# Layer 0's mixer takes x feature-major from the host, and squares the later token rows behind the value copies

## The chip, the cores and the metric

One core of one Trainium2 chip. The metric is the device time of one execution in microseconds (us). The engines are TensorE (PE, with its weight loads as PEld), VectorE (DVE), ScalarE (ACT), GpSimd (POOL) and SyncE (SP), which here issues nearly all DMAs.

## What is computed

A decoder trunk of two layers over 1024 tokens of width 1024, float32. Each layer is a token mixer and a gated feed-forward part with a causal convolution, each behind an RMS norm and with a residual. The change touches the beginning of layer 0's mixer: the norm of x, and the projections to q, k and v of the attention.

```python
def rms_norm(x, g):
    xf = x.astype(jnp.float32)
    return xf * lax.rsqrt(jnp.mean(xf * xf, -1, keepdims=True) + EPS) * g.astype(jnp.float32)
...
    z = h @ w_in
    u, v, q, k, vb = jnp.split(
        z, [A_WIDTH, 2 * A_WIDTH, 2 * A_WIDTH + B_WIDTH, 2 * A_WIDTH + 2 * B_WIDTH], axis=-1)
...
    qh = rms_norm(heads(q), q_g)
    kh = rms_norm(heads(k), k_g)
    vh = heads(vb).astype(jnp.float32)
```

## The kernel before

A float32 product is made of three products of shorter numbers. `split` (L95) writes a high part (a cast, on ACT unless `hi` names another engine, L100) and a low part (the difference, on DVE, L101); `mm_tok` (L182, matmuls at L190) multiplies high by high, high by low and low by high. The norm's weight is folded into the projection's weights (`scaled`, L103, rows L105 on ACT and L106 on DVE), and the norm's factor of each token (`r0`, one column for each of the 8 tiles of 128 tokens) is applied to the projection's result.

`even` (L510) begins with a loop over the 8 token tiles. For each it loads 128 rows of x (L523), turns them with 8 transposes on PE into two PSUM banks (`pt`, L530), splits each bank into `hq` (L531, 4 x 128 columns for each of two groups `g`), and sums the squares of the rows on ACT (L536); POOL makes the factor from the sum (`inv_rms`, L140 and L141). In the tile 1 round the weights of head pair 0 are loaded and split (`load_qkv`).

`attention` (L643) loads the q and k norm weights into `gqk` (four DMAs, L647 and L648, two copies of each side by side), scales the q part (L649), and calls `project(0, wq0)`. `project` (L696) goes over the 8 token tiles: 24 matmuls make `pj` of 128 x 384 (q, k, v of two heads); ACT squares q and k (L712), DVE sums them by head (L714), POOL makes the factor `rq`, DVE applies it (L716), POOL multiplies by `gqk` (L718), ACT copies the values to `vN` (L720), which a DMA writes out (L721). POOL and DVE split q and k into `qs` and `ks`, PE turns them (`tq` L730, `tk` L738; one PSUM bank for both), ACT or DVE copy them out (`qT` L733, `kT` L739), and `unit` makes scores `sc` (L661), the softmax (L666 on DVE, L667 on ACT), its transposes `pP` (L681), their copy `pT` and the products with the values `po` (L689). In `pj`, tile n of head pair p is written `pj{p}{n}`; buffer numbers are left out in the profile.

Each engine works off its own instructions in the order in which a scheduler put them when the program was built; that order is in the program, and an instruction that waits holds up all behind it on its engine. SP issues DMAs in order too.

Of the kernel before, what the change touches and what calls it, by code (L numbers as in the profile page):

```python
# [9 lines left out]
F32 = mybir.dt.float32  # L10
# [3 lines left out]
AF = mybir.ActivationFunctionType  # L14
# [5 lines left out]
P = 128  # L20
# [30 lines left out]
def rows(t, n):  # L51
    return t[n * P : (n + 1) * P, :]
# [3 lines left out]
def trunk(ctx: ExitStack, tc: tile.TileContext, a, out):  # L56
# [41 lines left out]
    def split(dst, src, hi=None, lo=None):  # L98

        (hi or A.copy)(dst[0], src)  # L100
        (lo or V.tensor_sub)(dst[1], src, f32(dst[0]))  # L101
# [65 lines left out]
    def place(t, n):  # L167
        return [t[:, i, :, (n % 4) * P : (n % 4 + 1) * P] for i in range(2)]
# [340 lines left out]
    def even(gm_open):  # L509
        with ExitStack() as st:  # L510
# [8 lines left out]
            pq0 = par0.enter_context(tc.tile_pool(name="pq0", bufs=1, side="right", reuse_waits="tile"))  # L519
            with tc.tile_pool(name="nrm", bufs=1, reuse_waits="tile") as pool:  # L520
                for n in range(NT):
                    xt = pool.tile([P, D], F32, tag="x", bufs=3, name=f"x0{n}")
                    Q.dma_start(xt, rows(a["x"], n))  # L523
                    if n == 0:
                        Q.dma_start(g0, a["norm_mix_gT"])
                    for g in range(2):
                        pt = ps.tile([P, 4, P], F32, tag="pt", name=f"pt{n}{g}")
                        for j in range(4):
                            k = 2 * j + g
                            T.transpose(pt[:, j, :], xt[:, k * P : (k + 1) * P], ident)  # L530
                        split(place(hq[g][n // 4], n), pt)  # L531
                    if n == 1:
                        wq0 = load_qkv(0, wx)
                    h = pool.tile([P, D], F32, tag="h", bufs=2, name=f"h{n}")
                    ssq = small.tile([P, 1], F32, tag="ssq", name=f"ssq{n}")
                    A.activation(h, xt, AF.Square, accum_out=ssq)  # L536
                    inv_rms(ssq, 1, D, f"rn{n}", r0[:, n : n + 1])
            with tc.tile_pool(name="at", bufs=2, reuse_waits="tile") as at, \
                    tc.tile_pool(name="av", bufs=1, reuse_waits="tile") as av:
                return attention(ps, at, av, pq, pq0, par0, wx, wq0, masks, gm_open)  # L540

# [100 lines left out]

    def attention(ps, at, av, pq, pq0, par0, wx, wq0, masks, gm_open):  # L643

        gqk = pq.tile([P, 2, 2, 64], F32, name="gqk", bufs=1)
        for s in range(2):
            Q.dma_start(gqk[:, 0, s, :], a["q_g"].partition_broadcast(P))  # L647
            Q.dma_start(gqk[:, 1, s, :], a["k_g"].partition_broadcast(P))  # L648
        V.tensor_scalar(gqk[:, 0], gqk[:, 0], -0.125, None, op0=ALU.mult)  # L649
        gqk = gqk.rearrange("p a s c -> p (a s c)")  # L650
        mband, mboth = masks
# [43 lines left out]

        def project(p, ws=None, then=None):  # L696

# [7 lines left out]
            for n in range(NT):  # L705
# [11 lines left out]
                                       op0=ALU.mult, op1=ALU.mult)  # L717
                G.tensor_tensor(qn, qn, gqk, op=ALU.mult)  # L718
                vN.append(pq.tile([P, P], F32, tag="vN", bufs=3, name=f"vN{p}{n}"))
                A.mul(vN[n], pj[:, 256:384], rn)  # L720
                Q.dma_start(rows(vd, n), vN[n])  # L721
# [78 lines left out]

        made = project(0, wq0)
        for p in range(PAIRS):
# [404 lines left out]
def layouts(i):  # L1207
# [26 lines left out]
    def tiles(w):  # L1234
# [4 lines left out]
    return {n: c(v) for n, v in {  # L1239
        "x": A["x"][0],  # L1240
        "norm_mix_g": A["norm_mix_g"][1:],
        "norm_mix_gT": A["norm_mix_g"][0].reshape(KD, P).T,
# [40 lines left out]
```

## Time and profile before

| what | value |
|---|---|
| three timed runs | 2170.96, 2171.78 (median) and 2174.12 us |
| the profiled execution | 2173.38 us, of which 2171.7 us are the profile's span |
| PE busy | 2138.3 us, 98% of the span |
| DVE, ACT, POOL busy | 71%, 48%, 23% |

The profile names a group of instructions by line, engine, operation and tiles (out<-in). In a list by time the columns are start, duration, engine, line, operation, tiles, count, and in brackets how long the engine had been idle and what ended it. In a table by stretch of time each engine has its busy time and count; then come the clock that TensorE was granted, the share of the DMA engines, and GB/s. An instruction's time is that of the hardware's record; those of one engine overlap a little, so the distance of two starts can be shorter than a duration.

### The profile page before, as it was taken

Reading aid. Unit: us, or ns where it says so; the run is one execution under the profiler, and the core shown is the slowest. Engines: PE = TensorE matmul, PEld = TensorE weight load, DVE = VectorE, ACT = ScalarE, POOL = GpSimd, SP = SyncE. Lnnn points to the kernel's source line nnn. Section 1 sums busy time; section 2 is a strip of 40 time slices with the busy share of each in tenths; the row PEclk is TensorE's granted clock in tenths of the full one; section 3 lists DMA queues with packets and bytes.
Section 4 is the critical chain, followed back from the end, with each engine's and each line's share of the span. In section 5 each row is a group of like instructions: output and inputs, shape, how many; then the busy total and the mean of one; then the engine's idle time right before and its main releaser. Section 6 shows DMA issues by size and latency. Waiting matters only on the chain.

```text
span 2171.7 us, 29864 instructions
## 1 busy us (share of the span) xinstructions
PE 2138.3 (98%) x10508; PEld 1811.4 (83%) x10508; DVE 1533.7 (71%) x2451; ACT 1033.9 (48%) x1998; POOL 488.9 (23%) x519
## 2 busy tenths in 40 slices
PE   8999999999999999999999999999999999999999
PEld 7999988887888888878889888888788888888887
DVE  6566655577887888755577776667788878885554
ACT  6555545355444444444454455534544444444443
POOL 4444411012342434100020011110233424220000
PEclk9999999999999999999999999999999999999999
DMA  4122312655444444675563233386554444457555
GB/s 163 43 83 62 82 51 84 217 207 193 159 151 160 160 165 160 199 266 195 193 215 127 73 98 97 107 295 232 197 165 160 151 152 157 165 181 276 199 196 202
DMA packets 157254, 349.59 MB, mean 161 GB/s; under 512 B 17408, under 2 KB 54272, under 8 KB 156720
## 3 DMA queue, kind: packets, MB, share of 16 engines
q1 hardware_dynamic: 157104, 347.68, 47.6%
q8 instruction: 83, 1.36, 0.3%
q14 instruction: 67, 0.55, 0.1%
HBM read 239.02 MB, written 108.59 MB: 160 GB/s over the span
## 4 chain that ended last, share of the span: by engine, by line
PE 87%; DVE 4%; DMA 4%; ACT 3%; issue 1%; POOL 0%; SPq 0%; ACTq 0%; DVEq 0%; POOLq 0%
PE puB L290 11%; PE pgB L290 11%; PE pv L190 6%; PE pgC L290 6%; PE puC L290 6%; PE pj L190 5%; PE pdB L397 5%; PE pdC L397 5%; PE po L190 4%; PE pdO L397 4%; PE puA L290 3%; PE pgA L290 3%; PE pdP L397 2%; PE pdQ L397 2%; PE pu L190 2%; PE pBq L992 2%
## 5 line engine op out<-in xcount | busy, mean ns | idle before, releaser
L101 DVE TENSOR_TENSOR da<-ar,da 128x512 fp32r<-128x512 f32 x154 | 106.2, 690 | 160.2 <-ACT da L100 160.1
L100 ACT CAST da<-ar 128x512 fp32r<-128x512 f32 x154 | 95.9, 623 | 215.0 <-PE pdQ L397 91.8
L190 PE MATMUL po<-wo,hq 128*128 128x512 f32 x768 | 184.3, 395 | 1.2 <-ACT hq L100 1.2
L190 PEld LDWEIGHTS po<-wo,hq 128*128 128x128 f32 x768 | 141.6, 188 | 30.9 <-ACT hq L100 1.6
L190 PE MATMUL pv<-wv,hq 128*128 128x512 f32 (+2 forms) x768 | 139.8, 339 | 2.0 <-DVE b L1024 1.6
L397 PE MATMUL pdB<-dw,da 128*128 128x512 f32 x528 | 136.3, 391 | 2.4 <-ACT dw L100 1.7
L397 PE MATMUL pdC<-dw,da 128*128 128x512 f32 x528 | 135.8, 390 | 0.0
L190 PEld LDWEIGHTS pv<-wv,hq 128*128 128x128 f32 x768 | 118.9, 189 | 17.4 <-DVE b L1024 2.1
L397 PEld LDWEIGHTS pdB<-dw,da 128*128 128x128 f32 x528 | 98.6, 188 | 24.0 <-ACT dw L100 2.1
L190 PE MATMUL pj<-wq,hq 128*128 128x384 f32 x576 | 117.3, 346 | 0.2 <-ACT vN L720 0.2
L256 POOL TENSOR_TENSOR S1g<-rg 128x512 f32<-128x512 f32 x20 | 30.0, 1498 | 382.9 <-DMA wsd<-D 249.7
L397 PEld LDWEIGHTS pdC<-dw,da 128*128 128x128 f32 x528 | 99.1, 188 | 20.5
L101 DVE TENSOR_TENSOR dw<-wr,dw 128x512 fp32r<-128x512 f32 x154 | 105.6, 686 | 8.2 <-ACT dw L100 7.7
L140 POOL TENSOR_SCALAR rn<-ssq 128x1 f32<-128x1 f32 x24 | 9.6, 399 | 452.2 <-ACT h L148 246.0
L397 PE MATMUL pdO<-dw,da 128*128 128x512 f32 x396 | 102.3, 389 | 0.2 <-DVE dw L101 0.2
L190 PEld LDWEIGHTS pj<-wq,hq 128*128 128x128 f32 x576 | 100.3, 191 | 0.5 <-ACT vN L720 0.4
L100 ACT CAST dw<-wr 128x512 fp32r<-128x512 f32 x154 | 95.0, 617 | 11.9 <-DMA wr<-in_w_dn 5.0
L397 PEld LDWEIGHTS pdO<-dw,da 128*128 128x128 f32 x396 | 74.3, 188 | 15.9 <-DVE dw L101 0.6
L319 DVE SCALAR_TENSOR_TENSOR t<-g,cw,t 128x1022 f32<-128x1022 f32 x44 | 76.6, 1742 | 0.1
L318 DVE SCALAR_TENSOR_TENSOR t<-g,cw,t 128x1023 f32<-128x1023 f32 x44 | 60.2, 1368 | 16.3 <-ACT t L317 16.3
L303 DVE TENSOR_TENSOR g<-g,s1g 128x512 f32<-128x512 f32 x22 | 16.2, 737 | 76.7 <-ACT s1g L302 76.7
L320 ACT ACTIVATE t<-t 128x1024 f32<-128x1024 f32 x44 | 46.7, 1061 | 32.5 <-DVE t L319 32.5
(1073 smaller groups left out, 5458.7 us busy)
## 6 DMA issues: line engine op xcount, KB each, us to landing
ar<-actd SPq DMA_DIRECT2D x70, 512.0 KB, 3.6
rd<-in_w_down SPq DMA_DIRECT2D x44, 512.0 KB, 3.7
wsd<-D SPq DMA_DIRECT2D x88, 256.0 KB, 2.5
rg<-in_w_gate SPq DMA_DIRECT2D x42, 512.0 KB, 3.6
ru<-in_w_up SPq DMA_DIRECT2D x42, 512.0 KB, 4.7
wr<-wsd SPq DMA_DIRECT2D x40, 512.0 KB, 4.3
actd<-t SPq DMA_DIRECT2D x66, 256.0 KB, 2.2
wr<-in_w_dn SPq DMA_DIRECT2D x30, 512.0 KB, 4.6
```

The source lines that it names most:

```text
L100: (hi or A.copy)(dst[0], src)
L101: (lo or V.tensor_sub)(dst[1], src, f32(dst[0]))
L140: G.tensor_scalar(r, ssq, 1.0 / n, EPS, op0=ALU.mult, op1=ALU.add)
L190: T.matmul(o, L[i], R[jj][:, sl], start=(k == 0 and (ii, jj) == PASSES[0]), stop=(k == nk - 1 and (ii, jj) == PASSES[-1]))
L256: G.tensor_tensor(sums[name], x, y, op=op)
L290: T.matmul(o, L[ii][:, j * P : j * P + P], right[p][:, jj, j, :], skip_group_check=more, start=(not more and j == 0 and (ii, jj) == PASSES ...
L303: V.tensor_add(C22, C22, s1)
L318: V.scalar_tensor_tensor(t[:, 1:], g[:, : S - 1], w(1), t[:, 1:], op0=ALU.mult, op1=ALU.add)
L319: V.scalar_tensor_tensor(t[:, 2:], g[:, : S - 2], w(0), t[:, 2:], op0=ALU.mult, op1=ALU.add)
L320: A.activation(t, t, AF.Silu)
L397: T.matmul(o, L[ii][:, t * P : t * P + P], R[jj], skip_group_check=more, start=start and not more and (ii, jj) == PASSES[0], stop=stop and ...
L992: T.matmul(o, L[ii][:, j * P : j * P + P], right[p][:, jj, j, :], skip_group_check=more, start=(not more and j == 0 and (ii, jj) == PASSES ...
```

## The change

The host hands over a second copy of x, `x_T`, in the form that `hq` needs. The first loop loads a tile of it (`xf`, L544) and splits it straight from the loaded tile; the transposes and their PSUM banks are gone. For tiles 0 to 3 the high part of the second group is a copy on POOL. The token rows of x are loaded as well (`token_rows`, L535), since the sums of squares need them: those of tiles 0 to 2 are squared in the loop, in place; those of tiles 3 to 7 wait in memory that head pair 1 uses later (`xk`, `xq`), and `rest` puts their squares behind the copy of the values of tile n - 3 in `project`. The q and k norm weights are loaded once each, into one copy (`gains`), and the multiplication on POOL (now L744) reads them for both heads through an operand that repeats.

```diff
             with tc.tile_pool(name="nrm", bufs=1, reuse_waits="tile") as pool:
+                Q.dma_start(g0, a["norm_mix_gT"])
+                xk = pq.tile([P, 4, S], F32, tag="kT", bufs=1, name="xk")
+                xq = pq.tile([P, 2, S], F32, tag="qR", bufs=1, name="xq")
+
+                def home(name, tag, bufs):
+                    return pool.tile([P, D], F32, tag=tag, bufs=bufs, name=name)
+
+                def statistics(n, xt):
+                    ssq = small.tile([P, 1], F32, tag="ssq", name=f"ssq{n}")
+                    A.activation(xt, xt, AF.Square, accum_out=ssq)
+                    inv_rms(ssq, 1, D, f"rn{n}", r0[:, n : n + 1])
+
+                def token_rows(n):
+                    xt = home(f"x0{n}", "a", 6) if n < 3 else xk[:, n - 3] if n < 7 else xq[:, 1]
+                    Q.dma_start(xt, rows(a["x"], n))
+                    later.append(xt)
+                    if n < 3:
+                        statistics(n, xt)
+
+                later = []
                 for n in range(NT):
-                    xt = pool.tile([P, D], F32, tag="x", bufs=3, name=f"x0{n}")
-                    Q.dma_start(xt, rows(a["x"], n))
+                    xt = home(f"xf{n}", "a", 6) if n < 4 else home(f"xf{n}", "b", 2) if n < 6 else xq[:, n - 6]
+                    xf = xt.rearrange("p (g j t) -> p g j t", g=2, j=4)
+                    Q.dma_start(xf, a["x_T"][n])
+                    for g in range(2):
+                        split(place(hq[g][n // 4], n), xf[:, g], hi=G.tensor_copy if g and n < 4 else None)
                     if n == 0:
-                        Q.dma_start(g0, a["norm_mix_gT"])
-                    for g in range(2):
-                        pt = ps.tile([P, 4, P], F32, tag="pt", name=f"pt{n}{g}")
-                        for j in range(4):
-                            k = 2 * j + g
-                            T.transpose(pt[:, j, :], xt[:, k * P : (k + 1) * P], ident)
-                        split(place(hq[g][n // 4], n), pt)
-                    if n == 1:
                         wq0 = load_qkv(0, wx)
-                    h = pool.tile([P, D], F32, tag="h", bufs=2, name=f"h{n}")
-                    ssq = small.tile([P, 1], F32, tag="ssq", name=f"ssq{n}")
-                    A.activation(h, xt, AF.Square, accum_out=ssq)
-                    inv_rms(ssq, 1, D, f"rn{n}", r0[:, n : n + 1])
+                        token_rows(0)
+                    elif n > 1:
+                        if n == 2:
+                            gqk = gains(pq)
+                        token_rows(n - 1)
+                token_rows(NT - 1)
+
+            def rest(n, ins):
+                if n < 5:
+                    with tc.issue_after(ins.ins):
+                        statistics(n + 3, later[n + 3])
...
+    def gains(pq):
+
+        gqk = pq.tile([P, 2, 64], F32, name="gqk", bufs=1)
+        Q.dma_start(gqk[:, 0], a["q_g"].partition_broadcast(P))
+        Q.dma_start(gqk[:, 1], a["k_g"].partition_broadcast(P))
+        V.tensor_scalar(gqk[:, 0], gqk[:, 0], -0.125, None, op0=ALU.mult)
+        return gqk
...
-        gqk = pq.tile([P, 2, 2, 64], F32, name="gqk", bufs=1)
-        for s in range(2):
-            Q.dma_start(gqk[:, 0, s, :], a["q_g"].partition_broadcast(P))
-            Q.dma_start(gqk[:, 1, s, :], a["k_g"].partition_broadcast(P))
-        V.tensor_scalar(gqk[:, 0], gqk[:, 0], -0.125, None, op0=ALU.mult)
-        gqk = gqk.rearrange("p a s c -> p (a s c)")
...
-                G.tensor_tensor(qn, qn, gqk, op=ALU.mult)
+                both = qn.rearrange("p (a s c) -> p a s c", a=2, s=2)
+                G.tensor_tensor(both, both, gqk[:, :, None, :].to_broadcast([P, 2, 2, 64]), op=ALU.mult)
                 vN.append(pq.tile([P, P], F32, tag="vN", bufs=3, name=f"vN{p}{n}"))
-                A.mul(vN[n], pj[:, 256:384], rn)
+                got = A.mul(vN[n], pj[:, 256:384], rn)
+                if early:
+                    early(n, got)
...
-        made = project(0, wq0)
+        made = project(0, wq0, early=rest)
...
         "x": A["x"][0],
+        "x_T": A["x"][0].reshape(NT, P, 4, 2, P).transpose(0, 4, 3, 2, 1),
```

The order of the instructions changes on every engine up to the first matmul of head pair 1 (`pj` of pair 1, tile 0); from there on each engine has the same instructions in the same order as before. Three places of the changed part follow; a name's number tells buffers apart.

SP's queue at the start of the program, before: x's tiles 0 and 1 stand ahead of the weights of pair 0 (`wq00r` to `wq03r`).

```order
L523 DMA x_324<-in_x 128x1024
L525 DMA g_83<-in_norm_mix_gT 128x8
L523 DMA x_346<-in_x 128x1024
L110 DMA wq00r<-in_w_qkv 128x768
L110 DMA wq01r<-in_w_qkv 128x768
L110 DMA wq02r<-in_w_qkv 128x768
L110 DMA wq03r<-in_w_qkv 128x768
L523 DMA x_399<-in_x 128x1024
L647 DMA gqk<-in_q_g 128x64
```

The same place now (`xf` is a tile of `x_T`, `x` one of token rows):

```order
L521 DMA g_83<-in_norm_mix_gT 128x8
L544 DMA xf_327<-in_x_T 128x1024
L110 DMA wq00r<-in_w_qkv 128x768
L110 DMA wq01r<-in_w_qkv 128x768
L110 DMA wq02r<-in_w_qkv 128x768
L110 DMA wq03r<-in_w_qkv 128x768
L535 DMA x_365<-in_x 128x1024
L544 DMA xf_371<-in_x_T 128x1024
L544 DMA xf_377<-in_x_T 128x1024
L568 DMA gqk<-in_q_g 128x64
L569 DMA gqk<-in_k_g 128x64
L535 DMA x_387<-in_x 128x1024
```

The weights now stand behind one tile instead of two, the second tile behind the weights and the first token rows, and x goes through the queue twice.

On PE, where the turning of q and k of tile 0 begins, before: transposes of x stand between `tq`, `tk` and the scores (`pj_773` is tile 3, `pj_852` tile 4).

```order
L190 MATMUL pj_773<-wq_0_388,hq_85 128x384 x3
L738 MATMUL tk_590<-identr,ks_579 128x128 x3
L530 MATMUL pt_471<-ident,x_462 128x128 x4
L738 MATMUL tk_590<-identr,ks_579 128x128
L190 MATMUL pj_773<-wq_1_391,hq_87 128x384 x3
L530 MATMUL pt_485<-ident,x_483 128x128 x4
L190 MATMUL pj_852<-wx_364,hq_86 128x384 x3
```

Now `tq`, `tk` and the scores of tile 0 stand side by side between tiles 2 and 3 (`pj_604` and `pj_686`):

```order
L190 MATMUL pj_604<-wq_1_362,hq_87 128x384 x3
L758 MATMUL tq_489<-identr,qs_483 128x128 x2
L766 MATMUL tk_495<-identr,ks_484 128x128 x4
L686 MATMUL sc0n_504<-kT_440,qT_492 128x128 x2
L686 MATMUL sc0n_511<-kT_440,qT_492 128x128 x2
L190 MATMUL pj_686<-wx_335,hq_85 128x384 x3
```

What stood between the steps of one tile is gone from there.

On DVE, ahead of the copy of the keys of tile 1 (`kT_440<-tk_575`), now; the `hq` row has the loaded tile `xq` as input, and weights of pair 1 (`wq_0_1276` and on) stand in the row:

```order
L101 TENSOR_TENSOR qs_645<-qn_629,qs_645 128x2x64
L101 TENSOR_TENSOR hq_88<-xq,hq_88 128x4x128
L106 SCALAR_TENSOR_TENSOR wq_0_1276<-wq10r,g_83,wq_0_1276 128x384
L101 TENSOR_TENSOR ks_646<-qn_629,ks_646 128x2x128
L711 COPY pT0n_518<-pP0n_503 128x2x128
L106 SCALAR_TENSOR_TENSOR wq_1_1279<-wq10r,g_83,wq_1_1279 128x384
L739 TENSOR_REDUCE ss_713<-qn_711 128x4
L106 SCALAR_TENSOR_TENSOR wq_0_1284<-wq11r,g_83,wq_0_1284 128x384
L106 SCALAR_TENSOR_TENSOR wq_1_1287<-wq11r,g_83,wq_1_1287 128x384
L741 SCALAR_TENSOR_TENSOR qn_711<-pj_686,r_84,rq_715 128x256
L739 TENSOR_REDUCE ss_796<-qn_794 128x4
L767 CAST kT_440<-tk_575 128x16x32
```

Before, the same copy stood behind these:

```order
L101 TENSOR_TENSOR hq_88<-pt_492,hq_88 128x4x128
L101 TENSOR_TENSOR qs_810<-qn_798,qs_810 128x2x64
L101 TENSOR_TENSOR hq_86<-pt_506,hq_86 128x4x128
L739 CAST kT_539<-tk_666 128x16x32
```

The four weights of pair 1 (`wq10r`, `wq11r`), which before stood far ahead of it, have moved to just in front of this copy.

More of the change, by code (lines that the diff above doesn't have):

```diff
@@ L538, in even @@
+                token_rows(NT - 1)
[3 more added lines that the diff above has]
+                        statistics(n + 3, later[n + 3])
             with tc.tile_pool(name="at", bufs=2, reuse_waits="tile") as at, \
                     tc.tile_pool(name="av", bufs=1, reuse_waits="tile") as av:
-                return attention(ps, at, av, pq, pq0, par0, wx, wq0, masks, gm_open)
+                return attention(ps, at, av, pq, pq0, par0, wx, wq0, gqk, masks, rest, gm_open)
@@ L641, in u_proj, with attention @@
         proj512(ps, load_half(a["w_vu"][1], "wu", g0), "pu", consume)
-    def attention(ps, at, av, pq, pq0, par0, wx, wq0, masks, gm_open):
-        gqk = pq.tile([P, 2, 2, 64], F32, name="gqk", bufs=1)
-        for s in range(2):
-            Q.dma_start(gqk[:, 0, s, :], a["q_g"].partition_broadcast(P))
-            Q.dma_start(gqk[:, 1, s, :], a["k_g"].partition_broadcast(P))
-        V.tensor_scalar(gqk[:, 0], gqk[:, 0], -0.125, None, op0=ALU.mult)
-        gqk = gqk.rearrange("p a s c -> p (a s c)")
+    def attention(ps, at, av, pq, pq0, par0, wx, wq0, gqk, masks, rest, gm_open):
         mband, mboth = masks
@@ L694, in outputs, with project @@
                     ps.tile([P, 4, P], F32, tag="po", name="po" + name))
-        def project(p, ws=None, then=None):
+        def project(p, ws=None, then=None, early=None):
             ws = ws or load_qkv(p, wx)
```

## Prediction

> **What bounds the kernel now.** I read the page's busy shares first, then its chain of what ended last, by engine.
>
> ```profile
> PE 2138.3 (98%) x10508; PEld 1811.4 (83%) x10508; DVE 1533.7 (71%) x2451; ACT 1033.9 (48%) x1998; POOL 488.9 (23%) x519
> PE 87%; DVE 4%; DMA 4%; ACT 3%; issue 1%; POOL 0%; SPq 0%; ACTq 0%; DVEq 0%; POOLq 0%
> ```
>
> TensorE is the bound nearly everywhere. From the first matmul of head pair 1 on, all engines keep their order, so whatever that matmul gains or loses I carry to the end. Before, it started at 69.66 us:
>
> ```profile
> 69.66 5.30 PE L190 MATMUL pj<-wq,hq 128*128 128x384 f32 x20 [0.23 <-ACT vN L720]
> ```
>
> The table by stretch of time cuts the part ahead of it where PE's state changes.
>
> ```profile
> 0.00:15.10 15.10, 8.66 (x31) 7.84 (x32) 10.32 (x24) 10.70 (x19) 3.11 (x14) 1.00 0.78 261
> 15.10:42.70 27.60, 25.62 (x171) 24.84 (x169) 16.14 (x33) 17.99 (x37) 16.86 (x34) 1.00 0.47 166
> 42.70:49.80 7.10, 6.18 (x48) 5.37 (x49) 5.85 (x20) 5.07 (x17) 3.78 (x7) 1.00 0.01 2
> 49.80:66.30 16.50, 16.49 (x109) 16.11 (x107) 7.66 (x21) 8.92 (x23) 5.00 (x9) 1.00 0.13 36
> 66.30:69.70 3.40, 1.65 (x13) 1.40 (x13) 3.40 (x7) 1.72 (x5) 2.30 (x5) 1.00 0.81 223
> 69.70:73.10 3.40, 3.40 (x11) 3.40 (x12) 2.13 (x6) 0.00 (x0) 2.42 (x5) 0.54 0.69 222
> ```
>
> The columns after the stretch are PE, PEld, DVE, ACT, POOL, then PE's clock, DMA share, GB/s. PE is half idle at the start, full in the middle, and half idle once more just before 69.7, after which its clock falls to 0.54.
>
> **The transposes.** The groups by form (stretch 0 to 70) and PE's list by time give their price.
>
> ```profile
> L530 PE MATMUL pt<-ident,x 128*128 128x128 f32 x64 | 11.4, 312 | 6.7 <-DMA x<-in_x 5.5 <-DVE hq L101 1.2
> 16.37 0.60 PE L530 MATMUL pt<-ident,x 128*128 128x128 f32 x4
> 16.72 0.77 PE L190 MATMUL pj<-wq,hq 128*128 128x384 f32 x3
> 17.33 0.60 PE L530 MATMUL pt<-ident,x 128*128 128x128 f32 x4
> 19.86 1.90 PE L190 MATMUL pj<-wq,hq 128*128 128x384 f32 x10
> 24.23 0.66 PE L530 MATMUL pt<-ident,x 128*128 128x128 f32 x4 [1.25 <-DVE hq L101]
> 24.65 2.33 PE L190 MATMUL pj<-wx,hq 128*128 128x384 f32 x12
> 26.81 1.73 PE L190 MATMUL pj<-wq,hq 128*128 128x384 f32 x9
> ```
>
> Twelve projection matmuls take 26.81 - 24.65 = 2.16 us, 0.18 each. From 16.37 to 17.33 there are four transposes and three matmuls, so four transposes are worth 0.96 - 0.52 = 0.44 us. Of the 16 groups, 7 stand before the end of tiles 0 and 1 (21.76), in a stretch that something else sets; the 9 behind it are worth 9 x 0.44 = **4.0 us**. The wait of **1.25 us** at 24.23, for a bank that DVE was still reading, goes with the banks.
>
> **Tiles 0 and 1.** What sets this stretch now is the order of loads.
>
> ```profile
> wq03r<-in_w_qkv SPq DMA_DIRECT2D x1, 384.0 KB, 7.6
> 3.58 0.92 SPq L110 DMA_DIRECT2D wq03r<-in_w_qkv  x1
> 8.00:12.00 4.00, 3.01 (x12) 2.54 (x11) 3.06 (x6) 4.00 (x10) 0.75 (x2) 1.00 1.04 404
> ```
>
> The rows are the table of DMA issues (median us to landing), SP's list by time and one stretch. The last weights were issued at 3.58 and landed 7.6 later, at 11.2. One tile of x fewer stands ahead of them: 512 KB at 404 GB/s is 1.3 us, so they land at 9.9. Behind them come token rows 0, then `xf` of tiles 1 and 2, 1.3 us each: tile 2 lands at 13.8. The order makes tile 1 wait for that, since on DVE the second difference of tile 1 stands behind the first of tile 2. ACT's cast and two differences follow:
>
> ```profile
> L100 ACT CAST hq<-pt 128x512 fp32r<-128x512 f32 x16 | 9.3, 584 | 5.6 <-PE pt L530 5.4
> L101 DVE TENSOR_TENSOR hq<-pt,hq 128x512 fp32r<-128x512 f32 x16 | 11.0, 685 | 10.2 <-ACT hq L100 10.2
> ```
>
> 13.8 + 0.6 + 2 x 0.68 = 15.75, and then some 21 of the 24 matmuls of tile 1 remain: 15.75 + 21 x 0.18 = 19.55, where the trace had 19.86 + 1.90 = 21.76. That is **2.2 us** earlier. The doubled load of x (4 MB more) costs nothing beyond this: later tiles land every 2.6 us and PE needs 24 x 0.18 = 4.3 us for one. If the loads were as slow as the 261 GB/s of the first stretch, a pair would take 4.0 us and still be in time, but tile 2 would land 3 x 0.7 = 2 us later, which I keep as a bound.
>
> **New waits.** `tk` needs the bank that `tq` leaves, and the scores need `kT`; what stood between them is gone in tile 0.
>
> ```profile
> L733 ACT CAST qT<-tq 128x256 fp32r<-128x256 f32 x6 | 2.2, 363 | 0.6 <-PE tq L730 0.6
> L739 ACT CAST kT<-tk 128x512 fp32r<-128x512 f32 x3 | 1.8, 590 | 0.1
> PE tk L738 <- ACT qT L733: 0.6, 1, 0.6
> PE sc0n L661 <- ACT kT L739: 0.9, 2, 0.5
> ```
>
> The last two rows are from the table of who waited for whom (total, times, longest). Two copies with what lies around them, 0.75 us each: **-1.5 us**. From below it is nothing (the same waits cost 0.6 and 0.5 already), from above twice that, should tile 1 pay it too. What waits next is a burst of small work of tiles 1 to 3 before tile 5's `pj`; it lasted from the end of tile 4's `pj` to the start of tile 5's, 41.2 to 49.8, and has nearly the same instructions now:
>
> ```profile
> 40.27 0.94 PE L190 MATMUL pj<-wq,hq 128*128 128x384 f32 x4
> 49.82 2.32 PE L190 MATMUL pj<-wx,hq 128*128 128x384 f32 x12
> ```
>
> But in front of its first `kT` now stand twelve DVE rows (the eleven shown with the change, and one difference of `hq` before them), eight of them with both inputs in SBUF, while POOL works on q and k. The trace shows what that does:
>
> ```profile
> L106 DVE SCALAR_TENSOR_TENSOR wq<-wq02r,g,wq 128x384 fp32r<-128x384 f32 x2 | 1.1, 610 | 0.0
> L106 DVE SCALAR_TENSOR_TENSOR wq<-wq12r,g,wq 128x384 fp32r<-128x384 f32 x2 | 1.6, 863 | 0.0
> L718 POOL TENSOR_TENSOR qn<-qn,gqk 128x256 f32<-128x256 f32 x7 | 5.4, 768 | 4.5 <-DVE qn L716 3.8 <-ACT hq L100 0.7
> L100 POOL CAST ks<-qn 128x256 fp32r<-128x256 f32 x7 | 3.2, 451 | 0.2 <-PE tk L738 0.2
> L100 POOL CAST qs<-qn 128x128 fp32r<-128x128 f32 x7 | 2.3, 324 | 1.2 <-PE tq L730 0.9
> ```
>
> The same DVE operation took 610 ns where POOL was idle and 863 beside POOL's work: 0.25 us more. Five of eight rows so hit are **-1.3 us**; the ends are 0 and 8 x 0.25 = 2.0.
>
> The Trainium skill's page "SBUF — State Buffer", section "Who interferes with whom", speaks against this edit: a VectorE instruction with two SBUF inputs shares a read port with GpSimd's reads, as a lock held for a whole instruction. The changed differences read SBUF twice, where one input was a PSUM bank. The 0.25 us agrees in kind and is less than a whole POOL instruction; the lock in full is the second rival.
>
> **The other edits.** ACT loses four casts (4 x 0.58) and PE's banks; POOL gains four casts of 128x512, which no row shows: between 0.45 (the half as large `ks`) and 1.5 us (twice the multiplication by `gqk`); I take 0.7, nearer to the casts, and their results are wanted only 2 us after the high parts of the other group. At 1.5 us POOL's casts would still end before DVE comes to them. The squares of rows 3 to 7 (1.06 us each) stay on ACT, which was busy 18.0 of 27.6 us in the middle. Two `gqk` loads fewer: nothing waits for them. The multiplication with a repeating operand is priced in the fourth rival; I take no change.
>
> **The sum.** 2.2 + 4.0 + 1.25 - 1.5 - 1.3 = 4.65 us earlier. The profiled execution took 2173.38 (span 2171.7 and 1.7 around it), so it would be 2168.7; it stood 1.6 above the median of the runs, 2171.78, from which the forecast is **2167.1**. With the bounds: at best no new wait and no lock, 7.5, and 1.6 more if the fall of the clock at 69.7 goes (3.4 x 0.46): 9.1, or 2162.7. At worst loads 2 us late, waits 3.0, lock 2.0 and one more fall of the clock: 0.2 + 4.0 + 1.25 - 3.0 - 2.0 - 1.6 = -1.15, or 2172.9.
>
> **Rivals.** First, *the queues keep up*: no wait of those two takes effect, PE saves 7.5 to 9.1. For it: DVE was busy only 16.1 of 27.6 us and ACT 18.0; against it: the burst is a chain, not a matter of shares. About 2163.5; chance 0.28.
>
> Second, *the lock in full*: each of the eight DVE rows stands behind one whole POOL instruction, on average (768 + 451 + 324) / 3 = 0.51 us: 4.1 instead of 1.3, gain 1.85, 2169.9. Against it stands the 0.25. Chance 0.07.
>
> Third, *the clock falls in the burst too*. Before, 1.65 of 3.4 us busy, with no single wait over 0.9 (below), was followed by 3.4 us at 0.54. I expect the burst about 55% busy (4.5 of 8 us). A fall costs 3.4 x 0.46 = 1.6: gain 3.0, 2168.7. Against it: 6.18 of 7.1 us busy at 42.7 brought none. Chance 0.16.
>
> ```profile
> PE po0n L689 <- DVE pT0n L686: 0.9, 1, 0.9
> ```
>
> The Trainium skill's page "TensorE: Matmul & The Clock Gate", section "HAM oscillation — how this bites in real kernels", asks only that no idle gap be longer than about 3.4 us; by it the burst keeps its clock and the forecast stands. The row disagrees: no gap near that came before the fall at 69.7.
>
> Fourth, *slower*: the multiplication by `gqk`, whose operand now has a repeating axis, is on the way from `pj` to `tq` in all 32 tiles of the attention. A POOL product with a repeating operand took:
>
> ```profile
> L796 POOL TENSOR_TENSOR ot1n<-ot1n,cE 128x512 f32<-128x512 f32 x2 | 2.7, 1341 | 6.2 <-DVE cE L793 6.2
> ```
>
> Half of 1341 is 0.67 for 128x256, no more than the 0.77 of now. Should the repeating axis instead cost as much as these 512 columns, 0.57 more, up to 32 x 0.57 = 18 us would come, up to 2185. It makes the kernel slower than before from 4.65 / 32 = 0.15 us that PE feels for each tile. Chance 0.05.
>
> **Chances.** The forecast has 0.44, with its own range 2165.3 to 2168.8 (gains of 3.0 to 6.5). 0.2% is 4.3 us, about what a measurement of this kernel can tell: a gain above 4.3 is faster. Of the forecast 0.29 lies there, of the first rival all 0.28, of the third 0.02: faster 0.59. Same: 0.15 of the forecast, 0.14 of the third, 0.07 of the second: 0.36. Slower: 0.05, the fourth. The range 2162.5 to 2170.5 takes in the forecast, the first rival, the third and most of the second, and leaves out the fourth and loads or waits at their worst.
>
> **What would show it.** `pj` of tile 1 ends near 19.5 us, tile 4's near 35, and pair 1 begins near 65. Waits of PE for `qT` and `kT` of about 0.7 us stand near 25, and a longer one for `kT` near 37. DVE's differences of `hq` stay near 0.69 us alone and reach 0.9 beside POOL; the multiplication at L744 stays near 0.77. The prediction is wrong if pair 1 begins before 62 or after 68, or if the gain there is not there at the end.

## The result, and the profile after

The changed kernel took 2169.86 us (median of 20 runs, 2165.94 to 2174.54), the kernel before 2174.41 beside it (20 runs, 2170.96 to 2180.34): ratio 0.9977, 95% interval 0.9969 to 0.9984, or **4.55 us faster** (2174.41 - 2169.86). The forecast's gain was 4.65. Its 2167.1 lies 2.8 lower since it started from three runs whose median was 2.6 below that of the twenty.

The page of the kernel after: busy shares, and the chain that ended last by engine.

```profile
PE 2134.0 (98%) x10444; PEld 1807.7 (83%) x10444; DVE 1535.3 (71%) x2451; ACT 1032.5 (48%) x1994; POOL 492.6 (23%) x523
PE 89%; DVE 4%; ACT 2%; DMA 2%; issue 1%; POOL 1%; SPq 0%; DVEq 0%; ACTq 0%; POOLq 0%
```

PE lost 4.3 us of busy time; the shares say nothing more. PE's list by time of the kernel after (start, duration, what it waited for) goes by the landmarks of the forecast: tile 1's `pj`, the end of tile 4's, tile 1's scores, tile 5's `pj`, pair 1's first.

```profile
16.36 1.49 PE L190 MATMUL pj<-wx,hq 128*128 128x384 f32 x7 [1.98 <-DVE hq L101]
17.69 2.25 PE L190 MATMUL pj<-wq,hq 128*128 128x384 f32 x12
...
33.93 2.27 PE L190 MATMUL pj<-wq,hq 128*128 128x384 f32 x12
39.03 1.22 PE L686 MATMUL sc0n<-kT,qT 128*128 128x256 f32 x4 [2.12 <-DVE kT L767]
...
46.59 3.42 PE L190 MATMUL pj<-wx,hq 128*128 128x384 f32 x12
...
68.26 3.56 PE L190 MATMUL pj<-wq,hq 128*128 128x384 f32 x19 [0.23 <-ACT vN L746]
```

Tile 1 ends at 17.69 + 2.25 = 19.94 (before 21.76), tile 4 at 36.20 (before 41.2), tile 5 begins at 46.59 (49.82), pair 1 at 68.26 (69.66). The gain of 1.8, then 5.0 us shrinks to 3.2 and 1.4 again. The table by stretch of time of the kernel after, first by the forecast's stretches, then in windows of 3.41 us (PE's clock is the third number from the end):

```profile
15.10:36.20 21.10, 18.13 (x107) 17.64 (x108) 16.69 (x36) 16.23 (x36) 17.73 (x29) 1.00 0.91 349
36.20:46.60 10.40, 7.72 (x45) 7.09 (x44) 5.77 (x16) 5.62 (x16) 6.71 (x11) 0.62 0.27 89
...
35.27:38.68 3.41, 1.64 (x14) 1.50 (x12) 2.50 (x6) 0.47 (x1) 2.64 (x4) 1.00 0.80 269
38.68:42.10 3.42, 2.52 (x13) 2.23 (x14) 2.53 (x8) 1.60 (x6) 3.18 (x7) 0.50 0.23 85
42.10:45.51 3.41, 3.41 (x19) 3.21 (x17) 1.17 (x4) 2.47 (x9) 1.67 (x4) 0.50 0.01 2
45.51:48.92 3.41, 3.41 (x16) 3.41 (x15) 1.92 (x4) 1.08 (x3) 0.78 (x3) 0.50 0.12 33
48.92:52.33 3.41, 3.41 (x25) 3.41 (x25) 0.73 (x3) 0.07 (x1) 0.00 (x0) 1.00 0.24 68
65.99:69.40 3.41, 2.24 (x14) 2.11 (x15) 3.41 (x8) 0.77 (x2) 0.25 (x2) 1.00 0.69 176
69.40:72.81 3.41, 3.41 (x24) 3.41 (x23) 1.50 (x5) 0.34 (x2) 2.60 (x5) 1.00 0.59 189
```

Two things are to be seen. From 15.1 to 36.2 PE is no longer the one busy engine: POOL (17.7 of 21.1 us), DVE and ACT are as full. And in the burst (36.2 to 46.6) the clock stands at half for three windows, after a window in which PE was busy 1.64 of 3.41 us. In the kernel before the same table has:

```profile
42.57:45.98 3.41, 2.49 (x18) 2.21 (x19) 3.41 (x14) 2.64 (x10) 1.85 (x3) 1.00 0.00 0
66.46:69.87 3.41, 1.82 (x13) 1.57 (x14) 3.41 (x7) 1.56 (x5) 2.23 (x6) 1.00 0.77 209
69.87:73.28 3.41, 3.41 (x12) 3.41 (x12) 2.15 (x6) 0.00 (x0) 2.33 (x4) 0.51 0.67 215
```

The fall of the kernel before at 69.87 did not come after the change (2.24 us busy ahead of it instead of 1.82), so 1.4 us at pair 1's start are 3.1 at 80 us and 2.7 at the end of the profiled pair (2173.38 and 2170.67). One pair of profiles doesn't tell a gain any closer than that: at the first matmul of the output projection (`po<-wo`, 385.88 and 383.94) the distance is 1.9, and two profiled executions of the changed kernel itself differ by 1.0 there and by 1.6 at the end. The waits of PE in the first 45 us of the kernel after:

```profile
PE pj L190 <- ACT wx L105: 6.6, 1, 6.6
PE sc0n L686 <- DVE kT L767: 2.1, 1, 2.1
PE pj L190 <- DVE hq L101: 2.0, 1, 2.0
PE tk L766 <- POOL r L141: 0.9, 1, 0.9
PE sc0n L686 <- ACT kT L767: 0.7, 1, 0.7
PE tk L766 <- ACT qT L761: 0.6, 1, 0.6
```

And the groups that the forecast priced (0 to 70 us; the product by `gqk` over the whole span):

```profile
L101 DVE TENSOR_TENSOR hq<-xf,hq 128x512 fp32r<-128x512 f32 x12 | 8.3, 720 | 2.6 <-ACT hq L100 2.6
L570 DVE TENSOR_SCALAR gqk<-gqk 128x64 f32<-128x64 f32 x1 | 0.2, 195 | 1.7 <-DMA gqk<-in_q_g 1.7
...
L100 POOL CAST hq<-xf 128x512 fp32r<-128x512 f32 x4 | 2.8, 722 | 2.8 <-DMA xf<-in_x_T 2.7
...
L744 POOL TENSOR_TENSOR qn<-qn,gqk 128x256 f32<-128x256 f32 x32 | 24.9, 778 | 17.6 <-DVE qn L741 11.2 <-ACT wq L105 1.1 <-PE sc1n L686 0.9
```

### The profile page after: what moved, and what is told of

Same layout as the page of the kernel before. It is cut to its first block, busy times and chain, and to the rows that moved or that the text cites. A ratio compares the mean times of both kernels' runs of the same rounds, so it can differ in the third digit from the quotient of the medians.

```text
span 2169.0 us, 29722 instructions
## 1 busy us (share of the span) xinstructions
PE 2134.0 (98%) x10444; PEld 1807.7 (83%) x10444; DVE 1535.3 (71%) x2451; ACT 1032.5 (48%) x1994; POOL 492.6 (23%) x523
## 4 chain that ended last, share of the span: by engine, by line
PE 89%; DVE 4%; ACT 2%; DMA 2%; issue 1%; POOL 1%; SPq 0%; DVEq 0%; ACTq 0%; POOLq 0%
PE puB L290 11%; PE pgB L290 11%; PE pv L190 6%; PE pdB L397 6%; PE pgC L290 6%; PE puC L290 6%; PE pdC L397 5%; PE po L190 5%; PE pj L190 5%; PE pdO L397 4%; PE puA L290 3%; PE pgA L290 3%; PE pdP L397 2%; PE pdQ L397 2%; PE pu L190 2%; PE pBq L1020 2%
## 5 line engine op out<-in xcount | busy, mean ns | idle before, releaser
L320 ACT ACTIVATE t<-t 128x1024 f32<-128x1024 f32 x44 | 46.7, 1061 | 32.1 <-DVE t L319 32.1
```

The costliest lines, as they stand in the source:

```text
L320: A.activation(t, t, AF.Silu)
```

## The experiments

My first theory: PE's freed time is the gain, and DVE's queue (a wait for `gqk`'s load, pair 1's weights in front of `kT`) gives part of it back, the clock's fall being its consequence. Rivals: the clock is a cause of its own; POOL is what holds; the doubled load of x; the single load of `gqk`; the place of the squares. All ratios are to the kernel before, run beside each kernel on the same chip, with 95% intervals (5 to 12 executions of each kernel). The last five columns are from one profiled execution: the end of tile 4's `pj`, the starts of tile 5's and of pair 1's, windows of 3.41 us at half clock ahead of 75 us, and the start of the output projection (`po`). The scheduler moved some work across pair 1's start, so that column compares kernels only roughly; from 202 us on PE's order is the same in all, and the last column is a fair one, to the 1 us by which two executions of one kernel differ.

| kernel | median, us | ratio | tile 4 ends | tile 5 | pair 1 | half | po |
|---|---|---|---|---|---|---|---|
| before | 2174.4 | 1 | 41.2 | 49.8 | 69.7 | 1 | 385.9 |
| after | 2169.86 | 0.9977 (0.9969 to 0.9984) | 36.2 | 46.6 | 68.3 | 3 | 383.9 |
| after, again | 2169.95 | 0.9969 (0.9956 to 0.9982) | 36.2 | 46.7 | 68.4 | 3 | 383.0 |
| gqk_scale_late | 2169.46 | 0.9969 (0.9959 to 0.9979) | 35.5 | 45.9 | 67.8 | 3 | 382.2 |
| wts_late | 2171.70 | 0.9982 (0.9973 to 0.9991) | 38.3 | 44.7 | 66.0 | 3 | 385.9 |
| gqk_early | 2165.16 | 0.9952 (0.9939 to 0.9964) | 39.0 | 45.5 | 66.3 | 0 | 378.9 |
| both | 2167.09 | 0.9958 (0.9944 to 0.9972) | 38.1 | 44.5 | 66.4 | 1 | 380.5 |
| cast_act | 2164.65 | 0.9956 (0.9942 to 0.9971) | 34.5 | 43.3 | 62.8 | 2 | 379.3 |
| cast_early | 2166.56 | 0.9956 (0.9943 to 0.9970) | 37.0 | 43.9 | 63.5 | 0 | 378.8 |
| fill | 2172.65 | 0.9990 (0.9981 to 0.9998) | 37.9 | 47.5 | 68.6 | 2 | 383.2 |
| dummy_pt | 2171.61 | 0.9985 (0.9975 to 0.9995) | 38.0 | 44.9 | 65.7 | 0 | 381.7 |
| sq_loop | 2175.60 | 1.0006 (0.9996 to 1.0015) | 38.9 | 47.8 | 69.5 | 4 | 386.7 |
| gqk_alone | 2173.84 | 0.9991 (0.9981 to 1.0001) | 40.4 | 49.6 | 69.2 | 1 | 384.0 |
| x_once | 2167.94 | 0.9964 (0.9951 to 0.9976) | 38.1 | 44.4 | 65.5 | 1 | 381.1 |

**The changed kernel once more** (no edit).

> The changed kernel once more, beside which the other three of this group are read. Every theory expects the same ratio to the kernel before, 0.997 to 0.9985, that is 3 to 6.5 us less. The theories differ in what the profile of another execution shows: if the fall of the clock in the burst (10.3 us at half between 39 and 49 us in the first profile) comes from the burst itself, it stands there again for two or three windows; if it is chance, it is gone or elsewhere and the profiled time is then some 4 us less.

The same three windows at half clock stood in the burst, 38.8 to 49.1: the burst brings them, though not in every execution. Four of the changed kernel's 27 had a mean clock of 0.999, which has no room for three (0.0008 each, worked out below).

**One instruction moved: DVE's wait for gqk's load.**

```diff
-        V.tensor_scalar(gqk[:, 0], gqk[:, 0], -0.125, None, op0=ALU.mult)
...
+                sm = V.reduce_sum(ssq, heads(qn), axis=AX.X)
+                if p == 0 and n == 0:
+                    with tc.issue_after(sm.ins):
+                        V.tensor_scalar(gqk[:, 0], gqk[:, 0], -0.125, None, op0=ALU.mult)
```

> The changed kernel with one instruction moved: the scaling of gqk stands on DVE four places later, behind the sum of tile 0's squares; loads and everything else stay in their order, so PE starts near 6.6 us as in the changed kernel. Theory (DVE's wait for gqk's load holds tile 1): tile 1's pj waits 0.3 to 0.6 us in place of 2.0 and ends near 18.3, and if that shift also keeps the burst denser, less of it runs at half clock: ratio to the kernel before 0.995 to 0.9965. Rival (it was the order of the loads, that is PE's later start at 9.5 us, that kept the clock up when gqk was loaded first; the 1.5 us are absorbed by the burst): the wait goes, the windows at half clock stay three, ratio 0.997 to 0.998.

PE's waits in the first 45 us of this kernel:

```profile
PE sc0n L685 <- DVE kT L769: 2.2, 1, 2.2
PE tk L768 <- ACT qT L763: 1.4, 1, 1.4
PE pj L190 <- DVE hq L101: 1.0, 1, 1.0
```

Half of the wait of tile 1 went, tile 1 ended 1.1 us earlier (18.85), the wait of tile 0's `tk` grew from 0.9 to 1.4 (the profile names POOL's `r` for it before, `qT` here), and 0.5 us were left at pair 1's start; the ratio can't be told from the changed kernel's. The wait was real and is not what the time hangs on; the rival was right.

**gqk loaded first.**

```diff
                 Q.dma_start(g0, a["norm_mix_gT"])
+                gqk = gains(pq)
...
-                        if n == 2:
-                            gqk = gains(pq)
```

> The changed kernel with the two loads of gqk ahead of every x tile. Theory (on DVE the scaling of gqk stands ahead of the low parts of tile 1 and waits 1.7 us for its load): the wait of 2.0 us of tile 1's pj goes down to 0.3 to 0.6, tile 1's pj ends near 18.4 instead of 19.9, ratio to the kernel before 0.9970. Rival (the loads of x and the weights set the start, and two small loads ahead of them push all back): tile 0's pj starts 0.5 to 1 us later, tile 1's ends where it did, ratio 0.9977 to 0.998. Should the time won at the start be lost again in the burst behind tile 4, ratio 0.9977 although tile 1's pj ends earlier.

It gained, but not in the way that I expected: PE starts 2.9 us later, tile 1 ends at 23.3 instead of 19.9, and still tile 5 begins 1.1 us earlier. PE's first and sixth tile, and the two stretches that end and begin with them:

```profile
9.55 4.71 PE L190 MATMUL pj<-wx,hq 128*128 128x384 f32 x12 [9.55 <-ACT wx L105]
...
45.48 2.31 PE L190 MATMUL pj<-wx,hq 128*128 128x384 f32 x12
```

```profile
15.10:38.98 23.88, 21.15 (x124) 20.43 (x123) 17.59 (x37) 17.07 (x38) 19.93 (x33) 1.00 0.87 321
...
38.98:45.48 6.50, 4.92 (x44) 4.27 (x42) 4.31 (x15) 5.03 (x15) 4.17 (x8) 1.00 0.35 111
```

The burst lasts 6.5 us in place of 10.4, at full clock (mean clock 1.000 in all five executions). Of these 3.9 us PE's busy time makes 2.8 (7.7 to 4.9 us, for 45 and 44 instructions), which is mostly the clock, and PE's idle time 1.1. An earlier start of PE alone buys nothing here: tile 1's scores began at 38.82 without a wait, and at 39.03 behind a wait of 2.1 us in the changed kernel.

**Pair 1's weights behind tile 5's normalization, alone and with gqk first.**

```diff
+            if p == 1:
+                with tc.issue_after(after5[0].ins), tc.issue_after(after5[1].ins):
+                    ws = load_qkv(p, wx)
```

> The changed kernel with the splitting of pair 1's weights put behind tile 5's normalization, so that nothing of it stands ahead of the first kT copies on DVE. Theory (the queue of DVE keeps PE waiting for kT, and that idleness is what lowers the clock): the wait of 2.1 us for kT shrinks to 0.8 or less, the clock falls later or for fewer windows, pair 1 begins 1.3 us earlier at least and up to 5 us earlier if the clock stays; ratio to the kernel before 0.9955 to 0.9971. Rival one (the chain through POOL and ACT sets the kT copy anyway): the wait becomes one of 1.5 to 2 us for the same copy with POOL's power or sum as its cause, ratio 0.9975 to 0.998. Rival two (the clock falls from a burst that is half empty whatever the wait): the wait goes, 10 us at half stay, ratio 0.997 to 0.9973.

> The two edits (weights of pair 1 split later, gqk loaded first) together. Theory (two separate waits of PE on DVE's queue): the gains add, 1.5 us at the start and 1.3 us at kT, ratio 0.9963, and to 0.9945 if the clock holds in the burst. Rival (one chain, in which the later wait takes up what the earlier one gave): ratio as that of the better of the two alone, 0.997.

In `wts_late` the wait for `kT` fell as the theory said, and the time did not (the wait in the first 45 us, and two windows further on):

```profile
PE sc0n L686 <- DVE kT L772: 0.5, 1, 0.5
```

```profile
60.72:64.13 3.41, 1.56 (x13) 1.29 (x12) 3.10 (x6) 3.41 (x8) 1.17 (x3) 1.00 0.28 65
64.13:67.55 3.42, 3.26 (x16) 3.10 (x16) 3.42 (x8) 1.50 (x5) 1.21 (x3) 0.51 0.63 202
```

In the burst the theory held: it lasted 6.4 us (38.3 to 44.7) with no window at half clock (on another offset of the clock's grid, which may have its part in that), and pair 1 began 2.2 us earlier. The weights now end last in front of pair 1, where PE is idle instead, and the clock falls there for two windows, and for one at 26.6, behind tile 0's waits, which the changed kernel has too. What is refuted is that the gain reaches the end: the idle time and the fall moved to another place. Together with `gqk` first nothing adds.

**POOL's casts back on ACT, alone and with gqk first.**

```diff
-                        split(place(hq[g][n // 4], n), xf[:, g], hi=G.tensor_copy if g and n < 4 else None)
+                        split(place(hq[g][n // 4], n), xf[:, g], hi=None)
```

> The changed kernel with the four casts of hq's second group (tiles 0 to 3) back on ACT. Theory (POOL's casts are cheap and cost DVE little, and ACT has no room before tile 3): 4 x 0.6 us more on ACT, tile 1's and 2's pj 0.5 to 1 us later, ratio to the kernel before 0.9975 to 0.9985, that is within 1.5 us of the changed kernel. Rival one (POOL sharing SBUF's port with DVE costs much): DVE's differences of hq fall from 720 to about 690 ns, the kT wait shrinks by 1 us, ratio 0.9965 or better. Rival two (ACT is the queue that starts each tile): 2 us slower than the changed kernel, ratio 0.9987.

> The changed kernel with both edits that helped alone: the casts of hq's second group back on ACT, and the loads of gqk ahead of x. Theory (both act on one thing, the burst behind tile 4: POOL's queue is shorter, DVE's wait for gqk is gone, so PE is busier there and keeps its clock): the better of the two alone is about all there is, ratio to the kernel before 0.9945 to 0.9955, with the granted clock at full speed in the first 90 us. Rival (two separate savings, 4.8 us each): ratio near 0.9925. Other rival (the later start of PE, 9.5 us in place of 6.7, costs 2 to 3 us as soon as the burst is no longer what bounds): ratio 0.9965.

Neither the theory (a loss) nor the rivals' reasons fit `cast_act`. DVE's differences took 777 ns instead of 720, so the gain does not come from fewer meetings of DVE and POOL; DVE's wait for the factor `rq` that POOL makes fell (first row: the kernel after, second: `cast_act`, 0 to 50 us):

```profile
L741 DVE SCALAR_TENSOR_TENSOR qn<-pj,r,rq 128x256 f32<-128x256 f32 x5 | 2.4, 483 | 4.4 <-POOL rq L141 4.4
```

```profile
L741 DVE SCALAR_TENSOR_TENSOR qn<-pj,r,rq 128x256 f32<-128x256 f32 x5 | 2.4, 483 | 2.6 <-POOL rq L141 2.6
```

Tile 1's q and k were normalized at 22.93 us in place of 26.17 and tile 3's at 33.39 in place of 37.57. The scheduler also put tile 3's `pj` ahead of tile 0's `tk` on PE, so which of the two carries the gain stays open. In `cast_early`, where `tk` comes first again and PE starts 2.8 us later than in `cast_act`, tile 3 was at 37.28, the clock held in the burst, and the ratio (0.9956) is that of the two edits alone (0.9956 and 0.9952): one gain, not two, as the theory had it.

**Work for nothing in PE's gap, and the transposes put back.** Both add PE work whose results nobody reads: `fill` behind tile 1's `tk`, `dummy_pt` in the first loop.

```diff
+                if p == 0 and n == 1:
+                    with tc.issue_after(tr.ins):
+                        fill = ps.tile([P, 512], F32, tag="pt", name="fill")
+                        for j in range(12):
+                            T.matmul(fill[:, :384], tok(0, 0)[0], ws[0][0], start=(j == 0), stop=(j == 11))
```

```diff
                     for g in range(2):
+                        pt = ps.tile([P, 4, P], F32, tag="pt", name=f"pt{n}{g}")
+                        for j in range(4):
+                            T.transpose(pt[:, j, :], xf[:, g, j], ident)
```

> The changed kernel with twelve more matmuls of 128x384 on PE behind tile 1's tk, whose sums nobody reads (4 us of work, in a place where PE waits 2 us). Theory (what is lost in the burst is the clock, and the clock follows how much PE has to do in the window of 3.4 us before): the windows at half clock in the burst go, three of them of 1.7 us each, so 4 us of added work cost nothing or even gain: ratio to the kernel before 0.9955 to 0.9975. Rival (the clock falls whatever PE does there, or the burst is bound by DVE and ACT alone): the added work adds 2 to 4 us, ratio 0.9985 to 1.0.

> The changed kernel with the 64 transposes of x put back on PE, into banks that nobody reads: the gain from leaving PE's work out is taken away, the loads and the squares stay changed. Theory (the gain is PE's freed time in the first 40 us, 16 groups at 0.44 us or 7 us less what the waits take): 3 to 6 us slower than the changed kernel, ratio 0.9995 to 1.0005. Rival (PE waits for DVE and ACT anyway, and the gain is from loads and squares out of the way): the transposes fit in PE's gaps and keep its clock up, ratio 0.9965 to 0.998.

`fill` lost 2.8 us on the changed kernel's median, and the clock still fell, in the burst for one window instead of three:

```profile
41.49:44.90 3.41, 2.27 (x16) 1.69 (x17) 2.04 (x7) 2.53 (x7) 2.72 (x5) 1.00 0.01 2
44.90:48.31 3.41, 3.41 (x19) 3.41 (x19) 2.55 (x8) 2.75 (x8) 1.12 (x3) 0.50 0.07 19
```

The added matmuls took 2.3 us (38.4 to 40.8) and ended before the window in which PE was too little busy (a thin one, for short), so this is no proof that filling can't work; it didn't here. Its other window at half, from 17.6, stands ahead of them. `dummy_pt` lies between what theory and rival expected: all 64 transposes put back cost 1.75 us by the medians (2171.61 - 2169.86), and the intervals overlap. In the first 70 us they cost nothing: pair 1 began 2.6 us earlier than in the changed kernel, with no window at half clock. One came from 139.5 to 142.9, and still the profiled execution reached the output projection 1.3 and 2.2 us ahead of the two profiled ones of the changed kernel. So the loss shows in the medians alone; where it arises no profile here shows. The mean clock was 0.9982 in its 12 executions against 0.9973, about one window at half fewer; at the 1.1 us for a window that are worked out below, the transposes' own price would be about 3 us, of which the clock gave one back (an estimate). The scheduler put PE's instructions in another order than the changed kernel's up to some 180 us, so I can't lay the loss to the transposes alone.

**The second part of the change undone.**

```diff
-                    if n < 3:
-                        statistics(n, xt)
+                    statistics(n, xt)
...
-                if n < 5:
-                    with tc.issue_after(ins.ins):
-                        statistics(n + 3, later[n + 3])
+                return
```

> The changed kernel with all squares in the loop over tiles, that is without the second part of the change (squares of rows 3 to 7 behind the copies of values). Theory (ACT starts the tiles, and five squares of 1.06 us in front of its copies make them late): waits of PE for copies on ACT grow by 1 to 3 us in the first 40 us, ratio to the kernel before 0.9985 to 1.0. Rival (ACT has room, it was busy 16 of 21 us): ratio as that of the changed kernel, 0.997 to 0.998; it could also be better, 0.996, if the r that POOL makes of each square comes earlier to the waiting tk.

The whole gain is gone, 5.7 us against the changed kernel, more than the theory said. Two of its three thin windows, each with the one behind it:

```profile
25.10:28.51 3.41, 2.26 (x14) 2.00 (x15) 1.76 (x5) 2.98 (x7) 3.17 (x7) 1.00 1.02 406
28.51:31.93 3.42, 3.42 (x13) 3.42 (x12) 3.14 (x8) 3.42 (x10) 3.25 (x6) 0.50 0.98 369
38.75:42.17 3.42, 1.32 (x11) 1.12 (x10) 2.26 (x5) 0.84 (x2) 2.86 (x8) 1.00 0.31 108
42.17:45.58 3.41, 2.75 (x14) 2.15 (x13) 1.74 (x8) 2.30 (x7) 1.42 (x2) 0.50 0.00 0
```

With a square ahead of `kT` on ACT the first scores wait 0.9 instead of 0.7 us, not the 1 to 3 us more of the theory; but three windows ahead of 75 us get thin in place of one, and tile 4 ends 2.7 us later. In the first of them the changed kernel, on nearly the same grid, was busy 2.53 us instead of 2.26, and kept its clock. Here too the scheduler's order differs up to some 180 us: this is the price of the edit as it is built, not of five squares by themselves. The mean granted clock of its 11 executions was 0.9953, of the changed kernel's 27 it was 0.9973: two and a half windows at half more, 2.8 us at 1.1 us each, about half of what is lost.

**The third part alone, and x loaded once.** `gqk_alone` is the kernel before with this; `x_once` is the changed kernel in which the token rows are not loaded and `statistics` reads the feature-major tile.

```diff
-        gqk = pq.tile([P, 2, 2, 64], F32, name="gqk", bufs=1)
+        gqk = pq.tile([P, 2, 64], F32, name="gqk", bufs=1)
...
-                G.tensor_tensor(qn, qn, gqk, op=ALU.mult)
+                both = qn.rearrange("p (a s c) -> p a s c", a=2, s=2)
+                G.tensor_tensor(both, both, gqk[:, :, None, :].to_broadcast([P, 2, 2, 64]), op=ALU.mult)
```

> The kernel before with only the third part of the change: gqk loaded once, and POOL's multiplication reads it with a repeating axis. Theory (that part is worth nothing): POOL's multiplication 0.74 to 0.80 us as before, ratio to the kernel before 0.999 to 1.001. Rival (the repeating axis costs PE 0.15 us or more in each of 32 tiles): ratio 1.002 to 1.008.

> The changed kernel without the loads of x by token rows: the squares are taken of the feature-major tiles, so the sums are not those of the token rows; 8 loads of 512 KB fewer. Theory (loads set only the start of tile 0, which they reach first; 4 MB less behind it moves nothing that PE waits for, except gqk's load, that lands earlier): ratio to the kernel before 0.996 to 0.998, tile 1's wait for hq 0.3 to 1 us. Rival (the doubled read of x holds back the pair's weights, gqk and r): PE's waits in the first 45 us fall by 3 us or more, ratio 0.994 to 0.9955.

The product by a repeating operand in `gqk_alone` took what the plain one took in the kernel before (762 ns):

```profile
L717 POOL TENSOR_TENSOR qn<-qn,gqk 128x256 f32<-128x256 f32 x32 | 24.4, 762 | 15.4 <-DVE qn L714 7.9 <-PE tk L737 1.0 <-PE sc2n L659 0.9
```

That part is worth nothing that can be told (interval 0.9981 to 1.0001). In `x_once` tile 1's wait for `hq` went, and tile 2's `pj` waited 3.3 us for a copy on ACT in its place; the ratio is in the theory's range and within 2 us of the changed kernel. So 4 MB more of loads are not what the first stage hangs on.

## Why the prediction was right, and where it was not

The gain is right, 4.55 us for 4.65. That it is met to 0.1 us is luck: the interval of the ratio reaches from 3.5 to 6.7 us, and two terms missed with opposite signs. By its own steps:

- **Start, 2.2.** It was 1.8 at tile 1's end, but the cause was not the landing of tile 2's load (its cast on ACT began at 13.10): DVE stood 1.7 us at the scaling of `gqk` (L570), ahead of tile 1's low parts. And the term does not reach the end: `gqk_scale_late` ended tile 1 a further 1.1 us earlier for nothing that can be told, `gqk_early` 3.3 us later and was faster.
- **Transposes and bank, 4.0 + 1.25.** Between the ends of tiles 1 and 4 PE took 36.20 - 19.94 = 16.3 us instead of 19.4: 3.2 less, with 1.6 of new waits in it, so 4.8 came where 5.25 were priced. But as a price at the end this is **the step that failed**: "worth 9 x 0.44 = 4.0 us" took PE as the bound of a stretch in which POOL, DVE and ACT then were busy 77 to 84%. Put back, all 64 transposes cost 1.75 us by the medians, with overlapping intervals: no run shows that taking them out was worth 4 us at the end. By the estimate above it was about 3 at equal clock, and a part of that went again with the clock.
- **New waits, -1.5.** 0.9 and 0.7 us in tile 0, as priced; the first was laid to `qT`, and its last cause is POOL's `r`.
- **The burst, -1.3.** 10.4 us instead of 8.6 before: -1.8, at half clock for most of it, with a wait of 2.1 for `kT` at 36.9 to 39.0, where it was expected. The mechanism was wrong: `hq`'s differences took 720 instead of 685 ns, the weights' rows ahead of `kT` 605 to 635 (610 alone). Not 0.25 us for each row but the rows' number and a wait of 0.9 us for POOL's `rq` behind them made DVE late. The 863 ns that gave the 0.25 were a mean of two unlike rows, 1085 and 641 ns: the first began inside POOL's product by `gqk` (65.72 to 66.69), the second behind it. So a row that meets a large POOL instruction can be held up by some 0.5 us; the second rival had the price of such a row right, and its count wrong, for hardly a row ahead of `kT` was hit.
- **Other edits, 0.** The squares' place was named there and priced at nothing. `sq_loop` says that without it there is no gain at all (1.0006), about half of that by the clock. This is the second miss, of the opposite sign.
- **Third rival, the fall of the clock in the burst** (chance 0.16). It came, in both profiles, for three windows and not one; the fall at 69.87 went, which leaves two more than before in the profiled pair. Over all executions the mean granted clock was 0.9981 before (66) and 0.9973 after (27); a window at half lowers it by 3.41 x 0.5 / 2169 = 0.0008, so the changed kernel has one such window more. Its executions at 0.996 took 2171.97 us on average (6), those at 0.999 2167.91 (4): 1.1 us for a window. At equal mean clock, as it is rounded, it is 7.2 us faster than the kernel before at 0.998 (26 and 5 executions) and 5.6 at 0.999 (19 and 4).
- **Fourth rival, the repeating operand.** Refuted: 778 ns against 762, and `gqk_alone`.

The forecast called itself wrong if pair 1 began after 68: it began at 68.26, and by this test its account of the place was wrong while the sum was right. What the runs show in its place: the first stage after the change is bound by the chain through POOL, DVE and ACT, and by whether the clock holds in the burst. Three kernels, `cast_act`, `gqk_early` and `cast_early`, are 3 to 5 us faster than the changed kernel by their medians; which of them is best the intervals don't tell. Their mean clocks were 1.0000, 0.9988 and 0.9998 (in the order `gqk_early`, `cast_act`, `cast_early`) against 0.9973: at 1.1 us for a window that is, as an estimate, 3.8, 2.1 and 3.5 us beside the 4.7, 5.2 and 3.3 that they gained, so in two of them the clock is about the whole of it, in `cast_act` less than half. Which part of the change makes how much of the 4.55 stays open: undoing the squares' place takes all of it, putting the transposes back at most a part, the single `gqk` is worth nothing that can be told, and each of these edits also moves PE's order and the clock. Open stays too how much of `cast_act` is POOL's queue and how much PE's order, and how much of the clock's fall a run's offset (below) decides.

## What to carry to other kernels

Work taken from an engine that is nearly full is worth its time only until the next engines are as full: add up their busy time in the same stretch before pricing it. A step moved to another place in a queue has a price even if nothing is added or removed; here the whole gain hung on it. Where idle time lowers the clock, add up PE's busy time window by window, for gaps of 1 to 2 us are enough.

## What the runs showed of the hardware

In every profile the clock of TensorE fell and rose on one grid of 3.41 us: in `wts_late` at 26.65 and 64.20, 11 windows apart, in `sq_loop` at 28.51, 42.17 and 69.47, 4 and 8 apart. The grid's offset from the program's start differed from profile to profile (0.15 to 2.9 us), so one kernel can lose a window in one execution and not in the next. The Trainium skill's page "TensorE: Matmul & The Clock Gate", section "What's actually happening", says the same of the window: 3413 ns, free-running; these runs agree.

What fills a window is less than an idle gap. All 16 falls in the first 75 us of the 14 profiles came behind a window of the grid with PE busy 0.5 to 2.3 of 3.41 us; no window above 2.4 was followed by one, and of the windows between 1.87 and 2.3 some were. So the busy time is not the whole measure: the window of 1.87 us in the changed kernel (14.82 to 18.23), all of it projection matmuls, kept the clock, and that of 2.27 us in `fill`, most of it small transposes, lost it. Which work counts how much isn't isolated here. The longest single wait in the burst of the changed kernel was 2.1 us. The Trainium skill's page "TensorE: Matmul & The Clock Gate", section "HAM oscillation — how this bites in real kernels", asks for no gap longer than about 3.4 us; by it the clock would have stayed, and these runs disagree. Of the 16 falls 11 lasted one window, two lasted two, and three lasted three, in the burst of the changed kernel (both profiles) and of `gqk_scale_late`: two windows with PE busy 2.52 and 3.41 us in small tiles (38.68 to 45.51) were not enough to raise the clock; it rose after the third.

In the changed kernel the start runs at half as well, though the clock column says 1.00 there. In the 14 profiles the first record of the clock comes at 9.7 to 16.1 us, and the column is 1.00 ahead of it. Here it comes at 11.4, on the grid, 8 windows ahead of the fall at 38.7: tile 0's first twelve matmuls took 0.375 us each (6.63 to 11.13), the next twelve 0.186 (11.13 to 13.36).
